# Decoder layer: the down projection's parts moved between the pairs of the next gate-up block, seven of eight pairs in seven products, some operand sums made by DMA

## The chip, the cores and the metric

The kernel runs on one core of a Trainium2 chip. A core has a matrix engine (TensorE; PE in the profile, PEld for its weight loads), VectorE (DVE), ScalarE (ACT), GpSimd (POOL) and SyncE (SP), which work side by side and wait for one another through semaphores. DMA transfers are issued from an engine's queue and carried out by 16 DMA engines. SBUF is the working memory; matmuls write into PSUM, which is used here as eight banks of 128x512 float32.

The metric is the device time of one execution in microseconds. The kernel before took 1120.58 us, the median of three runs (1119.26 to 1120.66).

## The reference

One decoder layer on x of 256 tokens by 2048 in float32: a normalised input goes through one combined projection, two groups of heads (gated linear attention and sparse attention) make the mixer's output, an output projection adds it to x, and a SwiGLU FFN of width 5632 follows. Only the last lines matter here:

```python
h = x + jnp.concatenate([gla_out, nsa_out], axis=-1) @ w_out
m = rms_norm(h, ffn_norm_g)
return h + (jax.nn.silu(m @ w_gate) * (m @ w_up)) @ w_down
```

`w_gate` and `w_up` are 2048 x 5632, `w_down` is 5632 x 2048, all float32.

## The kernel before

**Precision.** A float32 matrix is used as a high part (`hi`, a copy into the matmul type, on ACT) and a low part (`lo`, the difference, on DVE). `in_parts` (L572) makes both: ACT at L573, then DVE at L574. A product of two such matrices takes three matmuls (hi hi, hi lo, lo hi) into one bank.

**The FFN in blocks.** The FFN's width is cut into 11 blocks of 512 columns. For each block `gate_up` (L972) makes the gate and up values of both token halves, and `down` (L1065) multiplies the block's activations by 512 rows of `w_down` and adds them to the residual `h_sb`. The 16 groups of 128 rows of `w_gate` and `w_up` are taken as eight pairs (a, b).

**Eight products or seven.** A pair is a 2x2 block product: two token halves by the groups a and b by the columns gate and up. Done plainly it takes eight products of a 128x128 tile of the tokens with a 128x512 tile of weights. For the pairs named in `SEVENS` (L877) it takes seven, in the way of Strassen and Winograd: token combinations (`forms`, made once by `pair_forms` and `late_forms`) meet weight combinations made anew for each block. Of the four weight tiles ga, gb, ua, ub that `load4` (L951) fetches, three are split into parts as they are (`w`; here called A), and four sums (called B) are made first: `s1` = (gb + ub, ua + ub) in one DVE instruction at L1004, `s2` in two more (L1005, L1006), then both are split. The first three products use A, the last four B. The products go into seven banks that gather over all such pairs; an ordinary pair needs an eighth. In blocks 2 to 10 six pairs are in sevens, and pairs 6 and 7 are ordinary (`ORDERS` at L883 gives their places, fourth and last).

After the last pair in sevens (`last7`) four of the banks are read out and combined (L1029 to L1033, the evacuation); after the last pair comes the epilogue (L1042 to L1045) with silu and the product of gate and up. The activations are then turned by `turn_act` (L1051): TensorE transposes into a bank, `in_parts` into `hi` and `lo`. `down` copies the residual into four banks at a time (L1072), adds 24 matmuls for each quarter of 512 output columns and copies back (L1084).

**The order.** The main loop (L1108) emits `gate_up(f)` and then `down(f - 1)`. The generators yield after each product, and `drive` (L96) lets queued side work (`urgent`) run at a set pace in between: the turn of block f - 1 starts after `last7` of block f (L1034). The order that is emitted is a priority: when the kernel is built a planner lays down the order on each engine, and it lets a later instruction go ahead where an earlier one would not be ready by its costs. On the chip every engine then runs in that fixed order.

**Buffers.** Tiles come from slots: `fraw` (3, loaded weights), `ftwo` (4, parts), `fsum` (3, sums), `f2` (6, epilogue and forms), and `g4` (23, tokens in parts, forms, residual, activations), which has existed since the kernel's start. A slot is reused when the last reader of its tile is done. All weights are loaded from SP's queue.

## Time and profile before

| | before |
|---|---|
| median of three runs | 1120.58 us |
| the profiled execution | 1121.38 us |
| its span, first to last instruction | 1119.7 us |
| granted TensorE clock | 0.998 |
| moved by DMA | 213.47 MB, 191 GB/s |

The profile comes from one execution of its own. Busy times are shares of the span, and a busy PE counts matmuls that lie in one another's pipeline; idle time of an engine that sets nothing costs nothing. The groups of the FFN are those of L985 (gate and up), L262 (used by down, and by earlier stages), L573 and L574 (parts), L1004 to L1006 (sums). The slices show where the FFN lies: it begins at about 430 us, after 15 of 40 slices, and from there DVE is busy nearly throughout.

```profile
PE   9999999999999999999999999999999999999998
DVE  6556779876588678999998989898998999898972
ACT  6644457544476486667685867667676767667682
DMA  7665553444853354575565556566574655665562
```

The line of chain by line names the two that carry the end:

```profile
PE bank L262 50%; PE bank L985 39%; PE bank L193 2%; DMA raw<-in_w_out_dram 1%; PE bank L523 1%; PE bank L829 1%; PE bank L1058 1%; PE bank L770 1%; DMA g<-in_x_dram 1%; DVE ftwo L574 0%; DVE lo L130 0%; ACT hi L129 0%; PE bank L686 0%; PE bank L395 0%; PE bank L773 0%
```

### The profile page before, as it was taken

The page shows a single profiled execution, that of the slowest core. Times are in us where ns is not written, and L with a number is a line of the kernel's source. Part 1 is how long each engine was busy: PE and PEld are TensorE (multiplying, and loading weights), DVE is VectorE, ACT ScalarE, POOL GpSimd, SP SyncE. Part 2 cuts the span into 40 slices and gives each one's busy share as a digit, 9 for nine tenths or more (in the row PEclk, how much of TensorE's full clock was granted, in tenths as well). Part 3 has the DMA queues.
Part 4 walks back from the last instruction along what each step waited for, and adds up shares of the span by engine and source line. Part 5 has one row for each costly group of instructions (what it writes and reads, how often), then busy time and mean ns, then how long its engine had stood idle before and what let it go on. Part 6 is the DMA issues. An engine that isn't in the chain of part 4 may idle for free.

```text
span 1119.7 us, 14387 instructions
## 1 busy us (share of the span) xinstructions
PE 1110.7 (99%) x5395; PEld 918.9 (82%) x5395; DVE 935.7 (84%) x1205; ACT 719.9 (64%) x956; POOL 28.5 (3%) x67
## 2 busy tenths in 40 slices
PE   9999999999999999999999999999999999999998
PEld 8888888998778787788888888888888888888886
DVE  6556779876588678999998989898998999898972
ACT  6644457544476486667685867667676767667682
POOL 3000000101000000000000000000000000000000
PEclk9999999999999999999999999999999999999999
DMA  7665553444853354575565556566574655665562
GB/s 266 209 197 179 187 184 116 156 151 152 281 207 113 115 187 150 188 252 193 189 232 186 191 192 220 190 224 206 170 261 152 227 187 190 223 225 189 182 232 76
DMA packets 110449, 213.47 MB, mean 191 GB/s; under 512 B 5109, under 2 KB 8217, under 8 KB 110378
## 3 DMA queue, kind: packets, MB, share of 16 engines
q1 hardware_dynamic: 110378, 212.54, 56.5%
q8 instruction: 42, 0.69, 0.2%
q14 instruction: 29, 0.24, 0.1%
HBM read 210.42 MB, written 2.10 MB: 190 GB/s over the span
## 4 chain that ended last, share of the span: by engine, by line
PE 96%; DMA 2%; DVE 1%; ACT 0%; issue 0%; SPq 0%; POOL 0%; ACTq 0%; DVEq 0%
PE bank L262 50%; PE bank L985 39%; PE bank L193 2%; DMA raw<-in_w_out_dram 1%; PE bank L523 1%; PE bank L829 1%; PE bank L1058 1%; PE bank L770 1%; DMA g<-in_x_dram 1%; DVE ftwo L574 0%; DVE lo L130 0%; ACT hi L129 0%; PE bank L686 0%; PE bank L395 0%; PE bank L773 0%
## 5 line engine op out<-in xcount | busy, mean ns | idle before, releaser
L985 PE MATMUL bank<-ftwo,g 128*128 128x512 f32 x1881 | 439.4, 392 | 1.0 <-DVE ftwo L574 0.8
L985 PEld LDWEIGHTS bank<-ftwo,g 128*128 128x128 f32 x1881 | 349.3, 188 | 74.1 <-DVE ftwo L574 2.3
L262 PE MATMUL bank<-hi,g 128*128 128x512 f32 (+1 forms) x1088 | 324.6, 377 | 0.0
L574 DVE TENSOR_TENSOR ftwo<-fraw,ftwo 128x1536 fp32r<-128x1536 f32 (+1 forms) x130 | 263.1, 2036 | 12.7 <-ACT ftwo L573 12.0
L573 ACT ACTIVATE ftwo<-fraw 128x1536 fp32r<-128x1536 f32 (+1 forms) x130 | 221.0, 1713 | 63.6 <-PE bank L985 28.7
L262 PE MATMUL bank<-ftwo,g 128*128 128x512 f32 x1056 | 241.6, 389 | 0.0
L262 PEld LDWEIGHTS bank<-ftwo,g 128*128 128x128 f32 x1056 | 198.1, 188 | 41.2
L262 PEld LDWEIGHTS bank<-hi,g 128*128 128x128 f32 x1088 | 192.9, 189 | 30.8 <-issue 1.7
L130 DVE TENSOR_TENSOR lo<-raw,hi 128x1024 fp32r<-128x1024 f32 (+3 forms) x125 | 152.0, 1223 | 78.6 <-ACT hi L129 78.1
L129 ACT ACTIVATE hi<-raw 128x1024 fp32r<-128x1024 f32 (+3 forms) x125 | 131.3, 1057 | 113.1 <-PE bank L262 78.7
L262 PE MATMUL bank<-lo,g 128*128 128x512 f32 (+3 forms) x544 | 195.2, 377 | 0.6 <-DVE lo L130 0.6
L573 ACT ACTIVATE ftwo<-fsum 128x1024 fp32r<-128x1024 f32 x122 | 128.2, 1059 | 92.0 <-DVE fsum L1004 44.8
L574 DVE TENSOR_TENSOR ftwo<-fsum,ftwo 128x1024 fp32r<-128x1024 f32 x122 | 147.9, 1219 | 22.4 <-ACT ftwo L573 22.4
L262 PEld LDWEIGHTS bank<-lo,g 128*128 128x128 f32 x544 | 99.1, 189 | 16.0 <-DVE lo L130 1.2
L1004 DVE TENSOR_TENSOR fsum<-fraw 128x1024 f32<-128x1024 f32 x61 | 74.3, 1219 | 0.7 <-DMA fraw<-in_w_up_dram 0.6
L1084 ACT COPY g<-bank 128x512 f32<-128x512 f32 x80 | 45.6, 585 | 42.1 <-PE bank L262 39.8
L1072 ACT COPY bank<-g 128x512 f32<-128x512 f32 x88 | 48.3, 590 | 0.9 <-DVE g L574 0.8
L193 PE MATMUL bank<-ident,g 128*128 128x128 f32 (+2 forms) x230 | 41.0, 276 | 1.9 <-DMA g<-in_x_dram 1.1
L1005 DVE TENSOR_TENSOR fsum<-fsum,fraw 128x512 f32<-128x512 f32 x61 | 41.9, 687 | 0.8
L573 ACT ACTIVATE g<-bank 128x512 fp32r<-128x512 f32 x50 | 29.6, 599 | 19.5 <-PE bank L829 8.7
L1006 DVE TENSOR_TENSOR fsum<-fsum,fraw 128x512 f32<-128x512 f32 x61 | 41.7, 684 | 0.1
L193 PEld LDWEIGHTS bank<-ident,g 128*128 128x128 f32 (+2 forms) x230 | 30.0, 142 | 12.5 <-ACT g L910 1.9
(205 smaller groups left out, 673.2 us busy)
## 6 DMA issues: line engine op xcount, KB each, us to landing
fraw<-in_w_down_dram SPq DMA_DIRECT2D x44, 1024.0 KB, 5.1
fraw<-in_w_gate_dram SPq DMA_DIRECT2D x86, 512.0 KB, 3.8
fraw<-in_w_up_dram SPq DMA_DIRECT2D x86, 512.0 KB, 4.8
raw<-in_w_in_dram SPq DMA_DIRECT2D x36, 1024.0 KB, 5.1
raw<-in_w_out_dram SPq DMA_DIRECT2D x16, 1024.0 KB, 5.1
raw<-in_w_in_dram SPq DMA_DIRECT2D x4, 1072.0 KB
g<-in_x_dram SPq DMA_DIRECT2D x7, 512.0 KB, 8.8
raw<-in_w_in_dram SPq DMA_DIRECT2D x3, 1056.0 KB, 11.3
```

The lines of the kernel that those rows point to most:

```text
L129: act(h[:, i:i + n], r[:, k + i:k + i + n], AF.Copy)
L130: TT(o[:, i:i + n], r[:, k + i:k + i + n], f32(h[:, i:i + n]), ALU.subtract)
L193: return nc.tensor.transpose(o, i, ident[:n, :n])
L262: last["mm"] = mm(bk[t], a[:, k, t * P:(t + 1) * P], m[:, off:off + w], start=(first_ and k == 0 and i == 0), stop=(end and k == 3 and i = ...
L573: act(hi, ps, AF.Copy)
L574: TT(lo, ps, f32(hi), ALU.subtract)
L985: mm(banks[q], x, m, start=new and i == 0, stop=todo[q] == 0)
L1004: TT(s1, r[:, 1:3], r[:, 3:4].to_broadcast([P, 2, 512]), ALU.add)
L1005: TT(s2[:, 0], s1[:, 1], r[:, 1], ALU.add)
L1006: TT(s2[:, 1], s2[:, 0], r[:, 0], ALU.add)
L1072: nc.scalar.copy(banks[i][t], h_sb[2 * m + i][:, t, :])
L1084: nc.scalar.copy(h_sb[n][:, t, :], banks[i][t])
```

## The change

In blocks 2 to 10 seven pairs are in sevens instead of six; only pair 7, which comes last, stays ordinary. Pair 6 therefore gets forms (`LATE`). For pairs 0, 3 and 6 of these blocks (`ADDED`) the sum `s1` is no longer made by DVE: `added_sums` loads gb and ua into a slot from POOL's queue, and a third DMA from that queue adds ub to both. These pairs load three tiles with `load4` instead of four.

For f from 2 to 9 `down(f - 1)` is no longer emitted after `gate_up(f)` but inside it, as `down_parts`: the turn of block f - 1 lies in the second pair, its first token half in the middle and its second at the end; the third, fourth, sixth and seventh pair each hold one quarter of down, as two halves (one for each token half, 12 matmuls), again in the middle and at the end. Each half takes one bank, with a copy in and a copy out. Blocks 0, 1 and 10 keep down after `gate_up`; in block 10 the turn starts after the first pair, and what is left of the side work is emitted after each `gate_up`.

The slots: `fraw` 3 to 4, `f2` 6 to 4, `fsum` 3 to 2, two new for `fadd`; `g4` 23 to 21, with two for the gate's tiles moved to a pool that is released before the FFN.

```diff
-    g4, g2, g1, small = slot(gp, "g4", 23, LINE), slot(s2p, "g2", 13), slot(s1p, "g1", 7), slot(s1p, "sm", 12)
+    g4, g2, g1, small = slot(gp, "g4", 21, LINE), slot(s2p, "g2", 13), slot(s1p, "g1", 7), slot(s1p, "sm", 12)
+
+    g4m = slot(s2p, "g4m", 2, LINE)
     def bank():
         n_tiles[0] += 1
 ...
     def gla_gate(lr):
-        dec["f"], dec["r"] = g4([4, S]), g4([4, S])
+        dec["f"], dec["r"] = g4m([4, S]), g4m([4, S])
         nc.gpsimd.memset(dec["r"], 0.0)
         for _ in range(20):
             yield
 ...
-    SEVENS = [(0, 2, 4), (0, 2, 4, 5)] + [(0, 1, 2, 3, 4, 5) for f in range(2, NFB)]
+    SEVENS = [(0, 2, 4), (0, 2, 4, 5)] + [(0, 1, 2, 3, 4, 5, 6)] * 9
+    ADDED = [(), ()] + [(0, 3, 6)] * 9
     EARLY = (0, 2, 4, 5)
-    LATE = {0: (1, 3)}
+    LATE = {0: (1, 3, 6)}
     OLD = (1, 3)
-    ORDERS = [OLD + (0, 5, 2, 4, 6, 7), (0, 1, 2, 3, 4, 6, 5, 7)] + [(0, 1, 2, 6, 3, 4, 5, 7)] * 9
+    ORDERS = [OLD + (0, 5, 2, 4, 6, 7), (0, 1, 2, 3, 4, 6, 5, 7)] + [(0, 1, 2, 3, 4, 5, 6, 7)] * 9
     forms = {}
     turned = set()
 ...
         fr = ctx.enter_context(tc.tile_pool(name="fr", bufs=1, reuse_waits="tile"))
         fs = ctx.enter_context(tc.tile_pool(name="fs", bufs=1, reuse_waits="tile"))
         fp = ctx.enter_context(tc.tile_pool(name="fp", bufs=1, reuse_waits="tile"))
-        fw["raw"], fw["two"] = slot(fr, "fraw", 3, LINE), slot(fp, "ftwo", 4, LINE)
-        g2, small = slot(fs, "f2", 6), slot(fs, "fm", 4)
-        fw["sum"] = slot(fs, "fsum", 3, LINE)
+        fw["raw"], fw["two"] = slot(fr, "fraw", 4, LINE), slot(fp, "ftwo", 4, LINE)
+        g2, small = slot(fs, "f2", 4), slot(fs, "fm", 4)
+        fw["sum"], fw["added"] = slot(fs, "fsum", 2, LINE), slot(fs, "fadd", 2, LINE)
     def load4(parts):
         r, at = fw["raw"]([4, 512]) if fw else weight("raw", 4, 512, 3, F32), 0
         for mat, k0, nk, c0 in parts:
-            nc.sync.dma_start(r[:, at:at + nk], mat[k0 * P:(k0 + nk) * P, c0:c0 + 512].rearrange("(k p) w -> p k w", p=P))
+            nc.sync.dma_start(r[:, at:at + nk], rows_of(mat, k0, nk, c0))
             at += nk
         return r
+
+    def rows_of(mat, k0, nk, c0):
+        return mat[k0 * P:(k0 + nk) * P, c0:c0 + 512].rearrange("(k p) w -> p k w", p=P)
+
+    def added_sums(a, c0):
+
+        s = fw["added"]([2, 512])
+        gb, ua, ub = (rows_of(m[0], k, 1, c0) for m, k in ((w_gate, a + 1), (w_up, a), (w_up, a + 1)))
+        nc.gpsimd.dma_start(s[:, 0:1], gb)
+        nc.gpsimd.dma_start(s[:, 1:2], ua)
+        nc.gpsimd.dma_start(s, ub.to_broadcast([P, 2, 512]), accum_op=ALU.add)
+        return s
     def two_parts():
         w = fw["two"]([2, 4, 512], F32R)
 ...
         in_parts(hi[:, :n], lo[:, :n], src)
         return [(hi[:, k], lo[:, k]) for k in range(n)]
-    def gate_up(fb, aTs, before):
+    def gate_up(fb, aTs, before, between=None):
         banks = {}
 ...
         order, sevens = ORDERS[fb], SEVENS[fb]
         last7 = max(sevens, key=order.index)
+        free_bank = all(pair in sevens for pair in order[:order.index(last7)])
         todo = dict.fromkeys((1, 5, 6, 7), 3 * len(sevens))
         todo.update(dict.fromkeys((2, 3, 4), 3 * len(sevens) + 6 * (8 - len(sevens))))
         todo[8] = 6 * (8 - len(sevens))
 ...
             if fb == 0 and at == len(OLD):
                 ffn_pools()
             a, b = 2 * pair, 2 * pair + 1
-            r = load4([(w_gate[0], a, 2, fb * FB), (w_up[0], a, 2, fb * FB)])
             if pair in sevens:
+                added = pair in ADDED[fb]
+                if added:
+                    s1 = added_sums(a, fb * FB)
+                r = load4([(w_gate[0], a, 2, fb * FB), (w_up[0], a, 1 if added else 2, fb * FB)])
                 w = parts_of(r[:, 0:3])
-                s1, s2 = fw["sum"]([2, 512]), fw["sum"]([2, 512])
-                TT(s1, r[:, 1:3], r[:, 3:4].to_broadcast([P, 2, 512]), ALU.add)
+                if not added:
+                    s1 = fw["sum"]([2, 512])
+                    TT(s1, r[:, 1:3], r[:, 3:4].to_broadcast([P, 2, 512]), ALU.add)
+                s2 = fw["sum"]([2, 512])
                 TT(s2[:, 0], s1[:, 1], r[:, 1], ALU.add)
                 TT(s2[:, 1], s2[:, 0], r[:, 0], ALU.add)
                 f = [tuple(forms[pair][:, i, j] for i in range(2)) for j in range(4)]
 ...
                 yield 2
                 product(3, f[3], w, 2)
                 yield 2
+                if between is not None and at in TURNS:
+                    for _ in range(3):
+                        next(before)
+                elif between is not None and at in DOWNS:
+                    yield from next(between)
                 hi_, lo_ = two_parts()
                 in_parts(hi_[:, 0:2], lo_[:, 0:2], s1)
                 in_parts(hi_[:, 2:4], lo_[:, 2:4], s2)
 ...
                 for q, x, k in ((5, f[0], 0), (7, f[2], 1), (6, f[1], 2), (4, tokens(a, 1), 3)):
                     product(q, x, w, k)
                     yield 2
+                if between is not None and at in TURNS:
+                    for _ in before:
+                        pass
+                elif between is not None and at in DOWNS:
+                    yield from next(between)
             else:
-                w = parts_of(r)
+                w = parts_of(load4([(w_gate[0], a, 2, fb * FB), (w_up[0], a, 2, fb * FB)]))
                 for q, t, m in ((2, 0, 0), (3, 0, 1), (4, 1, 0), (8, 1, 1)):
                     for j in range(2):
                         product(q, tokens(a + j, t), w, 2 * m + j)
                         yield 2
+            if between is None and before is not None and (at == 0 if free_bank else pair == last7):
+                urgent.append(before)
             if pair == last7:
                 q1, q7u, q5u, q57u = (g2([512]) for _ in range(4))
                 act(q1, banks[1], AF.Copy)
 ...
                 TT(q5u, banks[5], q7u, ALU.subtract)
                 TT(q7u, banks[7], q7u, ALU.add)
                 TT(q57u, banks[5], q7u, ALU.subtract)
-                if before is not None:
-                    urgent.append(before)
         if fb == 0:
             drain(urgent)
             rms(rf, ssh)
 ...
             TT(u_, banks[uq], u_, ALU.add)
             STT(g, u_, rf[:, t:t + 1], g, ALU.mult, ALU.mult)
             gs.append(g)
-        turns[fb] = turn_act(gs, aTs)
+        turns[fb] = turn_act(gs, aTs, 1 if fb in WITHIN else 6 if fb else 0)
     turns = {}
-    def turn_act(gs, aTs):
+    WITHIN = range(1, NFB - 2)
+    TURNS, DOWNS = (1,), (2, 3, 5, 6)
+
+    def down_parts(f0, aTs):
+
+        (ah, al), = aTs
+
+        def half(n, t, ws):
+            b = bank()
+            nc.scalar.copy(b, h_sb[n][:, t, :])
+            for k in range(4):
+                for i, (x, m) in enumerate(((ah, ws[k][0]), (ah, ws[k][1]), (al, ws[k][0]))):
+                    mm(b, x[:, k, t * P:(t + 1) * P], m, start=False, stop=(k == 3 and i == 2), skip_group_check=True)
+                yield 2
+            nc.scalar.copy(h_sb[n][:, t, :], b)
+
+        for n in range(NQ):
+            ws = parts_of(load4([(w_down[0], 4 * f0, 4, n * 512)]))
+            for t in range(NT):
+                yield half(n, t, ws)
+
+    def turn_act(gs, aTs, gap):
         hi, lo = g4([4, S], F32R), g4([4, S], F32R)
         aTs.append((hi, lo))
         for t in range(NT):
 ...
                     yield
             pv = p.rearrange("p (j s) -> p j s", j=4)
             in_parts(hi[:, :, ts], lo[:, :, ts], pv)
+            for _ in range(gap if t == 0 else 0):
+                yield
     def down(f0, aTs, last):
 ...
     drive([w_out_half(1)], 6)
     acts = []
+
+    def later_parts(f):
+        yield from down_parts(f, acts[f:f + 1])
+
     for f in range(NFB):
-        drive([gate_up(f, acts, turns.get(f - 1))], 2 if f == 0 else 3)
+        inner = f - 1 in WITHIN
+        drive([gate_up(f, acts, turns.get(f - 1), later_parts(f - 1) if inner else None)], 2 if f == 0 else 3)
+        drain(urgent)
         if f == NFB - 1:
             urgent.append(turns[f])
-        if f:
+        if f and not inner:
             drive([down(f - 1, acts[f - 1:f], False)], 3)
     drive([down(NFB - 1, acts[NFB - 1:], True)], 3)
```

## The prediction

> **What bounds the kernel now.** I read the page first, for the span and the engines' shares, then the chain that ended last.
>
> ```profile
> span 1119.7 us, 14387 instructions
> PE 1110.7 (99%) x5395; PEld 918.9 (82%) x5395; DVE 935.7 (84%) x1205; ACT 719.9 (64%) x956; POOL 28.5 (3%) x67
> PE 96%; DMA 2%; DVE 1%; ACT 0%; issue 0%; SPq 0%; POOL 0%; ACTq 0%; DVEq 0%
> ```
>
> TensorE sets the end: 96% of the chain is PE. But the change touches only the FFN, so the shares must be read there. One FFN block reaches from one copy at L1029 to the next. These are two of them from the timeline, and the stretches they mark (the table of stretches: length, then busy time and count of PE, PEld, DVE, ACT, POOL, clock, DMA share, GB/s).
>
> ```profile
> 563.00 0.58 ACT L1029 ACTIVATE f<-bank 128x512 f32<-128x512 f32 x1
> 625.17 0.58 ACT L1029 ACTIVATE f<-bank 128x512 f32<-128x512 f32 x1
> 512.00:563.00 51.00, 51.00 (x226) 42.23 (x225) 50.61 (x55) 34.46 (x37) 0.00 (x0) 1.00 0.51 165
> 563.00:625.17 62.17, 62.17 (x279) 51.27 (x278) 58.83 (x55) 43.42 (x46) 0.00 (x0) 1.00 0.60 203
> 998.00:1060.70 62.70, 62.70 (x282) 51.77 (x281) 59.41 (x55) 43.79 (x47) 0.00 (x0) 1.00 0.60 201
> ```
>
> A block takes 62.17 us, PE is busy in all of it, and DVE in 58.83 (95%): 3.3 us of slack. So a product removed shortens the block only if DVE, which makes the operands, keeps up.
>
> **The gain.** The pace of PE, from the down stage of that block:
>
> ```profile
> 573.09 21.93 PE L262 MATMUL bank<-ftwo,g 128*128 128x512 f32 x96
> ```
>
> 21.93/96 = 0.228 us a matmul. Blocks 2 to 10 turn a seventh pair from eight products into seven, three matmuls each: 9 x 3 x 0.228 = **6.2 us less**, 0.68 a block. A block can at best take 61.5.
>
> **What DVE has to do.** These DVE instructions ran back to back; the distance of the starts is the true cost, since recorded times overlap by about 0.09 us.
>
> ```profile
> 553.90 1.22 DVE L1004 TENSOR_TENSOR fsum<-fraw 128x1024 f32<-128x1024 f32 x1
> 555.03 0.68 DVE L1006 TENSOR_TENSOR fsum<-fsum,fraw 128x512 f32<-128x512 f32 x1
> 555.64 1.22 DVE L574 TENSOR_TENSOR ftwo<-fsum,ftwo 128x1024 fp32r<-128x1024 f32 x1
> 556.77 1.75 DVE L574 TENSOR_TENSOR ftwo<-fraw,ftwo 128x1536 fp32r<-128x1536 f32 x1
> 558.44 1.22 DVE L574 TENSOR_TENSOR ftwo<-fsum,ftwo 128x1024 fp32r<-128x1024 f32 x1
> 559.58 0.68 DVE L1005 TENSOR_TENSOR fsum<-fsum,fraw 128x512 f32<-128x512 f32 x1
> 560.18 1.22 DVE L574 TENSOR_TENSOR ftwo<-fsum,ftwo 128x1024 fp32r<-128x1024 f32 x1
> 561.31 0.68 DVE L1006 TENSOR_TENSOR fsum<-fsum,fraw 128x512 f32<-128x512 f32 x1
> 561.92 2.28 DVE L574 TENSOR_TENSOR ftwo<-fraw,ftwo 128x2048 fp32r<-128x2048 f32 x1
> 564.12 1.22 DVE L574 TENSOR_TENSOR ftwo<-fsum,ftwo 128x1024 fp32r<-128x1024 f32 x1
> ```
>
> A pair in sevens costs 1.13 (s1) + 0.60 + 0.61 (s2) + 1.67 + 2 x 1.13 = 6.27 us of DVE beside 21 x 0.228 = 4.8 of PE; an ordinary pair or a quarter of down costs 2.20 beside 24 x 0.228 = 5.5. So sevens starve PE and down feeds it; that is why the change puts down between pairs. The sum for a block: one seven more (+6.27), one ordinary pair less (-2.20), three s1 by DMA (-3 x 1.13): **+0.68, or 59.5 us of DVE in 61.5**. Slack falls from 3.3 to 2.0 us. ACT copies the same tiles first:
>
> ```profile
> L573 ACT ACTIVATE ftwo<-fraw 128x2048 fp32r<-128x2048 f32 x69 | 131.2, 1914 | 29.6 <-DMA fraw<-in_w_down_dram 17.0 <-PE bank L985 12.2 <-DMA fraw<-in_w_up_dram 0.4
> L573 ACT ACTIVATE ftwo<-fsum 128x1024 fp32r<-128x1024 f32 x122 | 128.2, 1059 | 92.0 <-DVE fsum L1004 44.8 <-DVE fsum L1006 27.7 <-PE bank L985 13.5
> L573 ACT ACTIVATE ftwo<-fraw 128x1536 fp32r<-128x1536 f32 x61 | 90.6, 1486 | 34.0 <-DMA fraw<-in_w_up_dram 17.5 <-PE bank L985 16.5
> ```
>
> It gains 1.49 + 2 x 1.06 - 1.91 = 1.7 us, to 45 of 61.5: no bound by its sum.
>
> **How far DVE can run ahead.** Operands lie in four `ftwo` slots, before and after. At the start of block 3's pairs (PE at 594.86) DVE sat idle for want of a slot:
>
> ```profile
> 594.86 5.38 PE L985 MATMUL bank<-ftwo,g 128*128 128x512 f32 x23
> 596.63 2.36 DVE L574 TENSOR_TENSOR ftwo<-fsum,ftwo 128x1024 fp32r<-128x1024 f32 x2 [2.91 <-ACT ftwo L573]
> 626.29 1.22 DVE L574 TENSOR_TENSOR ftwo<-fsum,ftwo 128x1024 fp32r<-128x1024 f32 x1
> ```
>
> By then it had written pair 0 and the first half of pair 1. That lead is gone 32.6 us later: the last sums of the sixth seven are ready at 627.5, and PE wants them after 6 x 4.8 + 5.5 less its last six matmuls, at 627.7. Six sevens in a row just fit.
>
> **Blocks 3 to 9: one stall, taken at 0.4 us each.** With down inside, the tight place is the start of a block. There DVE owes, ahead of the first down half, the block before's epilogue and the turn as well:
>
> ```profile
> L1030 DVE TENSOR_TENSOR f<-bank,f 128x512 f32<-128x512 f32 x11 | 7.5, 684 | 0.0
> L1042 DVE TENSOR_TENSOR f<-bank,f 128x512 f32<-128x512 f32 x22 | 15.0, 681 | 0.6 <-PE bank L985 0.6
> L1044 DVE TENSOR_TENSOR f<-bank,f 128x512 f32<-128x512 f32 x22 | 15.0, 682 | 0.0
> L1045 DVE SCALAR_TENSOR_TENSOR f<-f,rf,f 128x512 f32<-128x512 f32 x22 | 16.4, 744 | 0.0
> L574 DVE TENSOR_TENSOR g<-bank,g 128x512 fp32r<-128x512 f32 x50 | 33.8, 687 | 5.6 <-ACT g L573 4.7
> L573 ACT ACTIVATE g<-bank 128x512 fp32r<-128x512 f32 x50 | 29.6, 599 | 19.5 <-PE bank L829 8.7 <-PE bank L193 7.3 <-PE bank L1058 3.2
> L1072 ACT COPY bank<-g 128x512 f32<-128x512 f32 x88 | 48.3, 590 | 0.9 <-DVE g L574 0.8
> L1084 ACT COPY g<-bank 128x512 f32<-128x512 f32 x80 | 45.6, 585 | 42.1 <-PE bank L262 39.8
> ```
>
> Less the overlap of 0.09 each: the evacuation (L1030 to L1033) costs 4 x 0.59 = 2.4, the epilogue 4 x 0.59 + 2 x 0.66 = 3.7, the turn 1.2. Count from the last down half of a block (t = 0). PE: pair 7 to 5.5, pair 0 to 10.2, pair 1 with the turn's transposes (62.17 - 270 x 0.228 = 0.6) to 15.7, first part of pair 2 to 17.8; then the first half wants its weights and a bank. DVE, in program order: from about -3.2: evacuation 2.4, B0 2.26, A1 1.67, epilogue 3.7, sums of 1 (1.2, its s1 in the idle time before), B1 2.26, A2 1.67, sums of 2 2.3, first turn 0.6, weights of down 2.2 (A the three loaded matrices, B the four sums): 20.3 us, so the weights come at 17.1, or at 18.2 where s1 of pair 1 was not done ahead. The bank is worse: seven of eight hold products, so the turn and every half share the eighth. After the turn's last transposes that bank wants ACT 0.60, DVE 0.69 and the copy in, 0.59: 1.88 and hand-overs of some 0.1 each, against the 9 x 0.228 = 2.05 of PE work in between. With nothing in the way the stall is about 0.1; with a 2.20 us DVE instruction ahead it reaches 1.8. PE runs in the order laid down at build, so all that stands behind the half waits with it. I take 0.4, nearer the low end because the order can put ready sums of pair 2 ahead of the half. Block 2 has no epilogue in front: 0. The later turn-arounds of that bank (copy out 0.59, copy in 0.59 in 2.05 or 2.7 us) cost nothing unless ACT is inside a 1.9 us instruction; that is in the upper end. Seven blocks: **+2.8, from 0.7 to 12.6**.
>
> [...]
>
> **Block 10: +3.2.** Its down comes after the pairs, so seven sevens run in a row, with an epilogue and a turn in front. DVE from t = -3.2 to pair 7's operands: 2.4 + 2.26 + 2.9 + 3.7 + 2.26 + 1.2 + (6.27 + 5.14 + 6.27 + 6.27 + 5.14) + 2.2 = 46.0, so 42.8; PE wants them at 39.6. The down stage that follows gives nothing back, since there PE is the bound. By orders, 1.5 to 4.5.
>
> **At nothing.** The sum by DMA: POOL is idle in these blocks (0.00 above), and with two slots a sum can be started over 20 us ahead of its reader (from one such pair to the next is 3 x 4.8 + 5.5). These loads land in about 5 us (first row), and the adding one waits for two of them; the other rows are waits between 563 and 1060 us:
>
> ```profile
> fraw<-in_w_up_dram SPq DMA_DIRECT2D x86, 512.0 KB, 4.8
> PEld bank L985 <- DVE ftwo L574: 0.2, 1, 0.2
> ACT ftwo L573 <- DMA fraw<-in_w_up_dram: 14.1, 8, 2.1
> ```
>
> Two landings are 10 us, twice that still fits; beyond 20 the excess would be PE's, three times a block. It can't be below nothing: PE never waited for a sum's add. Traffic rises by 3 x 768 KB a block, 203 to about 244 GB/s. The fourth `fraw` slot lets SP issue earlier, which may shorten the 1.8 us a block that ACT waits for loads; PE waited 0.2 in all of them (second row), so nothing is gained. SP's queue is otherwise as before; on POOL's, an adding DMA that waits holds only other sums. Five fewer slots elsewhere (`f2`, `fsum`) and the two `g4` moved: the evacuation waits for the turn to free `f2`, which is earlier than it was; -1 to +1 for all of it. The late forms of pair 6 add to the first down:
>
> ```profile
> 513.33 0.68 DVE L933 TENSOR_TENSOR f<-g,g 128x512 f32<-128x512 f32 x1
> 516.20 0.28 DVE L894 TENSOR_TENSOR f<-f 128x128 f32<-128x128 f32 x1
> ```
>
> That is 0.6 + 4 x 0.2 + 0.6 (the low part) = 2.0 us of DVE where it is full (50.61 of 51.00 above), less one s1, with block 2's lead as cover; 0 to +1.
>
> **Sum.** -6.2 + 2.8 + 3.2 = -0.2. The profiled execution took 1121.38 (span 1119.7), 0.8 over the median 1120.58 of the runs; so 1121.2 for such an execution and **1120.4** for the median.
>
> **Rivals.**
> 1. *PE alone.* The planner puts turn, weights and copies where they fit, stalls stay at 0.1, block 10 loses 1.5: -6.2 + 0.7 + 1.5 = -4.0, **1116.6**. For it: DVE's sum fits; before, six sevens fit with 0.2 us to spare and PE hardly waited. Against: four slots make DVE wait somewhere in a block (2.9 us above), and only 2.0 are left.
> 2. *The one bank.* The first half waits for it behind DVE in every block, others behind ACT. From 0.75 us a block on the kernel is slower (-6.2 + 3.2 + 7 x 0.75 = +2.2); at 1.2 and block 10 at 3.5 it is +5.7, **1126.3**. For it: 1.88 us of chain in 2.05, DVE 97% full. Against: DVE's order is planned, and ready sums can fill PE.
> 3. *The sums come late.* POOL's issues or the adding transfer take over 20 us; at 0.5 us for each of 27 pairs, +13.5, **1134**. Against: the landings above. [...]
>
> **Chances.** Forecast (1118.2 to 1122.8) 0.35; rival 1 0.34; rival 2 0.27; rival 3 0.04. A measurement tells some 0.2% (2.2 us) from no change, so faster 0.34, same 0.35, slower 0.31. The range 1115.5 to 1127.0 takes in rival 1 and most of rival 2; the forecast's own is 1118.2 to 1122.8.
>
> **What would show it.** 27 matmuls fewer; blocks 2 to 9 at 61.5 (rival 1), 61.9 (forecast) or above 62.6 (rival 2), with PE's gaps at L1072's copies or at the first weights of down; block 10 with PE waiting for `ftwo` by some 3 us; DVE at 96 to 97% in a block; adding DMAs landing well ahead of their sums' readers. I am wrong if block 10 runs without a gap, if PE waits at every half, or if DVE's instructions themselves get longer beside POOL.

## The result, and the profile after

The changed kernel took 1127.67 us (median of four runs, 1126.02 to 1129.83), the kernel before 1120.62 beside it: a ratio of 1.0066 (95% interval 1.0046 to 1.0087). It is slower by 7 us where no change was forecast, and just outside the range. The profiled execution is the slowest of the four, 1129.83 at a granted clock of 0.997; two others, at 1.000, took 1126.02 and 1126.74. The page's first lines and its chain:

```profile
span 1128.1 us, 14557 instructions
PE 1113.8 (99%) x5368; PEld 912.4 (81%) x5368; DVE 947.7 (84%) x1229; ACT 735.9 (65%) x975; POOL 93.4 (8%) x148
PE 91%; DMA 3%; DVE 3%; ACT 1%; issue 1%; SPq 0%; POOL 0%; ACTq 0%; DVEq 0%
```

5368 matmul records instead of 5395: the 27 are gone. Yet PE's share of the chain fell from 96% to 91%, and DMA, DVE and ACT stand in it now. To see where, I cut both spans at the copies of bank 1 out of the last seven (L1029 before, L1062 after), counted the matmuls between them, and took 0.2266 us (the common distance of two starts) off for each. What is left is the time "over", transposes included:

| stretch | before: length, matmuls, over | after: length, matmuls, over |
|---|---|---|
| FFN's start to block 0's copy | 27.76, 114, 1.93 | 30.00, 118, 3.26 |
| to block 1's copy | 49.80, 213, 1.54 | 52.74, 209, 5.38 |
| to block 2's | 61.28, 266, 1.01 | 80.78, 344, 2.83 (two downs) |
| blocks 3 to 9, each | 62.2, 270, 1.02 | 62.2 (two of 62.5), 267, 1.70 (two of 2.0) |
| to block 10's | 62.22, 270, 1.03 | 46.51, 187, 4.13 |
| from there to the end | 54.67, 232, 2.10 | 54.33, 231, 1.99 |

The balance of the two profiled executions: 27 x 0.2266 = 6.1 us gained; 5.2 lost in blocks 0 and 1 (8.64 over against 3.47), 7.2 in blocks 2 to 9, 3.1 in block 10; FFN's start 0.8 earlier and the end 0.1 shorter. Together +8.4, and the spans differ by 8.4. So the whole gain went back inside the very blocks that the change shortens, and what makes the kernel slower are the two ends: the start of the FFN and block 10.

Some of these stretches of the changed kernel (block 3, block 5, up to block 10's copy, and three pieces of the start; columns as in the prediction):

```profile
586.84:649.33 62.49, 62.47 (x277) 50.66 (x275) 58.56 (x56) 45.23 (x48) 7.13 (x9) 1.00 0.73 226
711.87:774.08 62.21, 62.21 (x277) 50.66 (x275) 59.69 (x57) 45.25 (x49) 7.11 (x9) 1.00 0.77 241
1022.91:1069.41 46.50, 44.65 (x196) 35.31 (x195) 46.03 (x48) 29.26 (x30) 3.59 (x4) 1.00 0.66 199
440.00:450.00 10.00, 10.00 (x44) 7.95 (x43) 9.14 (x9) 4.88 (x4) 2.02 (x2) 1.00 1.08 315
450.00:460.00 10.00, 7.83 (x34) 5.63 (x33) 8.03 (x9) 7.65 (x7) 0.00 (x0) 1.00 0.94 327
460.00:466.00 6.00, 4.58 (x12) 3.32 (x13) 6.00 (x5) 0.78 (x1) 0.00 (x0) 0.72 0.47 146
```

**Inside the blocks** PE seems busy throughout (62.21 of 62.21), since the records of matmuls overlap: one by itself lasts 0.39 us (L1000 at 1022.78), and the common distance of two starts is 0.2266. The table of waits between 586 and 1023 us, seven blocks, shows what the busy share hides (in total, times, longest):

```profile
POOL fadd L971 <- DMA fadd<-in_w_up_dram: 116.9, 21, 7.5
DVE fsum L1024 <- DMA fraw<-in_w_up_dram: 8.3, 7, 2.1
PEld bank L1094 <- ACT bank L1091: 7.6, 22, 0.6
DVE ftwo L576 <- ACT ftwo L575: 7.6, 15, 0.6
```

The third row is the one that counts: TensorE's weight loads for a down half waited 22 times, three a block, for ScalarE's copy of the residual into the half's bank (L1091). Before, no such row existed. DVE has 59.69 of 62.21 us of work and waits little. POOL's waits hold only other sums.

**At the start** the timeline of PE has three gaps, where the waits are for operands:

```profile
451.17 7.25 PE L1000 MATMUL bank<-ftwo,g 128*128 128x512 f32 x30 [0.71 <-DVE ftwo L576]
459.89 0.73 PE L1000 MATMUL bank<-ftwo,g 128*128 128x512 f32 x2 [1.46 <-ACT ftwo L575]
462.05 6.21 PE L1000 MATMUL bank<-ftwo,g 128*128 128x512 f32 x19 [1.43 <-DVE ftwo L576]
```

From 458.42 to 462.05 PE worked 0.73 us, and then the granted clock fell: 0.72 over 460 to 466 is one stretch of 3.41 us at half, which costs 1.7 of the 5.2 in this execution. The other 3.5 repeat: in the profiled executions of experiment 2 and of the first two kernels of experiment 6, which start the FFN in the same way, blocks 0 and 1 were 6.8 to 6.9 over without a stretch at half clock there (in that of experiment 3 even 9.0). The operands were late because their loads were. DMA issues between 433 and 466 us, after and then before (count, size, median us to landing):

```profile
fraw<-in_w_up_dram SPq DMA_DIRECT2D x8, 512.0 KB, 9.3
fraw<-in_w_gate_dram SPq DMA_DIRECT2D x7, 512.0 KB, 8.8
fadd<-in_w_up_dram POOLq DMA_DIRECT2D x2, 512.0 KB, 10.6
```

```profile
fraw<-in_w_gate_dram SPq DMA_DIRECT2D x6, 512.0 KB, 4.1
fraw<-in_w_up_dram SPq DMA_DIRECT2D x6, 512.0 KB, 4.9
```

The loads that blocks 0 and 1 need took twice as long. In the same time POOL fetched the first two sums, whose first reader, in block 2, runs at 526.67 us; and a fourth `fraw` slot lets SP issue one load more ahead. The DMA engines were full, with a share of 1.08 and 0.94 above; the same two stretches before:

```profile
440.00:450.00 10.00, 10.00 (x45) 8.01 (x44) 9.97 (x9) 5.95 (x6) 0.00 (x0) 1.00 0.65 210
450.00:460.00 10.00, 10.00 (x46) 8.12 (x45) 10.00 (x9) 5.72 (x5) 0.00 (x0) 1.00 0.71 250
```

**Block 10** has three gaps between 1059 and 1066 us, each behind ACT's copy of a late sum:

```profile
1059.25 4.66 PE L1000 MATMUL bank<-ftwo,g 128*128 128x512 f32 x19 [0.64 <-ACT ftwo L575]
1064.49 0.74 PE L1000 MATMUL bank<-ftwo,g 128*128 128x512 f32 x2 [0.57 <-ACT ftwo L575]
1065.86 6.45 PE L1000 MATMUL bank<-ftwo,g 128*128 128x512 f32 x27 [0.64 <-ACT ftwo L575]
```

There DVE is busy 46.03 of 46.50: that stretch is bound by it.

### The profile page after: what moved, and what is told of

It is laid out like the page before. It is cut to its first block, busy times and chain, and to the rows that moved or that the text cites. A ratio compares the mean times of both kernels' runs of the same rounds, so it can differ in the third digit from the quotient of the medians.

```text
span 1128.1 us, 14557 instructions
## 1 busy us (share of the span) xinstructions
PE 1113.8 (99%) x5368; PEld 912.4 (81%) x5368; DVE 947.7 (84%) x1229; ACT 735.9 (65%) x975; POOL 93.4 (8%) x148
## 4 chain that ended last, share of the span: by engine, by line
PE 91%; DMA 3%; DVE 3%; ACT 1%; issue 1%; SPq 0%; POOL 0%; ACTq 0%; DVEq 0%
PE bank L264 34%; PE bank L1000 33%; PE bank L1094 16%; PE bank L195 2%; DVE ftwo L576 2%; DMA fraw<-in_w_up_dram 2%; DMA raw<-in_w_out_dram 1%; PE bank L525 1%; PE bank L831 1%; PE bank L1110 1%; PE bank L772 1%; ACT ftwo L575 0%; DMA g<-in_x_dram 0%; DVE fsum L1024 0%; DVE lo L132 0%
## 5 line engine op out<-in xcount | busy, mean ns | idle before, releaser
L1000 PE MATMUL bank<-ftwo,g 128*128 128x512 f32 x1854 | 443.3, 393 | 6.2 <-ACT ftwo L575 4.0
L1000 PEld LDWEIGHTS bank<-ftwo,g 128*128 128x128 f32 x1854 | 346.2, 188 | 83.2 <-ACT ftwo L575 8.0
L576 DVE TENSOR_TENSOR ftwo<-fraw,ftwo 128x1536 fp32r<-128x1536 f32 (+1 forms) x130 | 259.2, 1999 | 13.1 <-ACT ftwo L575 13.0
L1094 PE MATMUL bank<-ftwo,g 128*128 128x512 f32 x768 | 188.4, 394 | 0.2 <-ACT bank L1091 0.2
L575 ACT ACTIVATE ftwo<-fsum 128x1024 fp32r<-128x1024 f32 x113 | 118.2, 1054 | 55.2 <-DVE fsum L1024 26.9
L576 DVE TENSOR_TENSOR ftwo<-fsum,ftwo 128x1024 fp32r<-128x1024 f32 x113 | 136.4, 1219 | 6.0 <-ACT ftwo L575 5.9
L1096 ACT COPY g<-bank 128x512 f32<-128x512 f32 x64 | 37.7, 588 | 64.5 <-PE bank L1094 64.5
L264 PE MATMUL bank<-ftwo,g 128*128 128x512 f32 x288 | 66.2, 390 | 0.0
L1024 DVE TENSOR_TENSOR fsum<-fraw 128x1024 f32<-128x1024 f32 x43 | 52.5, 1220 | 10.2 <-DMA fraw<-in_w_up_dram 10.1
L969 POOL DMA_DIRECT2D fadd<-in_w_gate_dram x27 | 15.8, 585 | 399.7 <-DVE ftwo L576 395.8
L1027 DVE TENSOR_TENSOR fsum<-fsum,fraw 128x512 f32<-128x512 f32 x70 | 48.1, 687 | 0.5
L971 POOL DMA_DIRECT2D fadd<-in_w_up_dram x27 | 33.2, 1231 | 142.3 <-DMA fadd<-in_w_up_dram 142.3
```

The lines of the kernel that those rows point to most:

```text
L264: last["mm"] = mm(bk[t], a[:, k, t * P:(t + 1) * P], m[:, off:off + w], start=(first_ and k == 0 and i == 0), stop=(end and k == 3 and i = ...
L575: act(hi, ps, AF.Copy)
L576: TT(lo, ps, f32(hi), ALU.subtract)
L971: nc.gpsimd.dma_start(s, ub.to_broadcast([P, 2, 512]), accum_op=ALU.add)
L1000: mm(banks[q], x, m, start=new and i == 0, stop=todo[q] == 0)
L1024: TT(s1, r[:, 1:3], r[:, 3:4].to_broadcast([P, 2, 512]), ALU.add)
```

## The experiments

The theory at this point has three parts, each with its place: sums fetched too early (start), the one bank (blocks 2 to 9), DVE (block 10). Its rivals: fewer slots or more traffic as such for the start, DVE instead of the bank inside the blocks. A time without a ratio is that of one execution, beside a kernel before of 1119.2 to 1119.4 on the same chip. In a kernel with added lines the copy into the bank (L1091) has a later number.

**1. Early sums.** Both `fadd` slots are held by dummy tiles until block 0's epilogue, so POOL's first loads can't start sooner.

```diff
+        fw["hold"] = [fw["added"]([2, 512]) for _ in range(2)]
+        for t in fw["hold"]:
+            nc.gpsimd.memset(t[:, 0, 0:1], 0.0)
 ...
+        if fb == 0:
+            for t in fw.pop("hold"):
+                nc.gpsimd.tensor_copy(t[:, 0, 0:1], gs[0][:, 0:1])
```

> Two tiles hold both fadd slots until block 0's epilogue, so the first sums by DMA start at about 470 us and not at 433. Theory 'early loads' (they crowd the first weights of the FFN, DMA share 1.08 and 0.94 between 440 and 460 us): PE's time over its matmuls in blocks 0 and 1 falls from 8.6 us to about 4 (before: 3.5) and the kernel gains 3 to 5 us, to about 1123.5. Rival 'slots' (fewer f2 and fsum slots delay blocks 0 and 1): no change, 1126 to 1129. The blocks after that stay at 62.2 us by both.

Measured: 1124.30 us, ratio 1.0045 (1.0028 to 1.0062). Over in blocks 0 and 1: 4.34 instead of 8.64, no stretch at half clock; blocks 3 to 9 are as before the hold. By the ratios the hold is worth 0.2%, some 2.4 us. Its loads and PE between 433 and 466 us:

```profile
fraw<-in_w_gate_dram SPq DMA_DIRECT2D x8, 512.0 KB, 4.2
fraw<-in_w_up_dram SPq DMA_DIRECT2D x7, 512.0 KB, 4.5
```

```profile
457.80 8.48 PE L1003 MATMUL bank<-ftwo,g 128*128 128x512 f32 x36 [1.51 <-ACT ftwo L575]
```

The landings are back at 4.2 and 4.5 us with the fourth `fraw` slot still there: it was the sums. One gap of 1.51 us for an operand remains, which the kernel before hasn't.

**2. The bank's copy in.** The half starts its bank with its first matmul instead of onto the residual, so the residual is missing from the result.

```diff
-            nc.scalar.copy(b, h_sb[n][:, t, :])
 ...
-                    mm(b, x[:, k, t * P:(t + 1) * P], m, start=False, stop=(k == 3 and i == 2), skip_group_check=True)
+                    mm(b, x[:, k, t * P:(t + 1) * P], m, start=(k == 0 and i == 0), stop=(k == 3 and i == 2), skip_group_check=True)
```

> The halves of down in blocks 2 to 9 start their bank without the residual (left out of the result), so no copy in stands between two users of the one free bank. Theory 'one bank': the gaps of 0.05 to 0.16 us at three half starts of a block, and the slower matmuls behind them, go: block period from 62.2 to about 61.7. Rival 'DVE': the halves start where DVE lets them, period stays at 62.2.

Measured: 1122.55 us. The inner blocks are 61.51 to 61.57 us long, 1.01 to 1.06 over, as before the change, and no wait of PE is left in them. So all of the 0.66 us a block hangs on that copy, and over blocks 2 to 9 it is 6.2 of the 7.2 us. DVE has the same work in a shorter block, and it suffices.

**3. DVE's work.** From block 2 on the second sums are left out, 14 DVE instructions a block (14 x 0.6 = 8.4 us).

```diff
-                s2 = fw["sum"]([2, 512])
-                TT(s2[:, 0], s1[:, 1], r[:, 1], ALU.add)
-                TT(s2[:, 1], s2[:, 0], r[:, 0], ALU.add)
+                s2 = s1
```

(blocks 0 and 1 keep theirs)

> From block 2 on the second sums are left out (the parts are made from s1 again), 1.2 us of DVE less for each pair in sevens, 8.4 us a block. Theory 'one bank': inner blocks stay near 62.2 us, as DVE was not their bound; block 10 loses its 3.1 us of extra, since there DVE was. Rival 'DVE sets the inner blocks too': their period falls to about 61.6.

Measured: 1126.66 us. The inner blocks got longer, 62.5; block 10 lost its gaps (1.25 over instead of 4.13). A stretch inside the blocks, and PE's waits there:

```profile
711.00:773.00 62.00, 61.83 (x273) 50.02 (x274) 50.57 (x42) 43.96 (x47) 7.12 (x9) 1.00 0.78 239
```

```profile
PEld bank L1096 <- ACT bank L1093: 11.3, 34, 0.6
```

DVE had 11 us to spare, and TensorE waited at the bank 34 times instead of 22. In block 5 the half at 32.3 us now has six matmuls between it and the half before, where the changed kernel has eight and no wait; why the built order came out so was not tested. DVE bounds block 10 and none of the blocks 3 to 9.

**4. Block 10 with six pairs in sevens**, in the order of before, with no sums by DMA.

```diff
-    SEVENS = [(0, 2, 4), (0, 2, 4, 5)] + [(0, 1, 2, 3, 4, 5, 6)] * 9
-    ADDED = [(), ()] + [(0, 3, 6)] * 9
+    SEVENS = [(0, 2, 4), (0, 2, 4, 5)] + [(0, 1, 2, 3, 4, 5, 6)] * 8 + [(0, 1, 2, 3, 4, 5)]
+    ADDED = [(), ()] + [(0, 3, 6)] * 8 + [()]
```

> Block 10 as in the kernel before (six pairs in sevens, its old order, no sums by DMA). Theory 'seven in a row starve PE there': block 10 loses 3.1 us of gaps and takes three matmuls more (0.7), so 2.4 us less, about 1125.2. Rival 'it is the epilogue and the turn in front of it': they stay, and the gain is under 1 us.

Measured: 1127.76 us, ratio 1.0074 (1.0059 to 1.0089): nothing gained where the theory said 2.4 us. Over up to the copy fell from 4.13 to 1.48, but the last stretch rose from 1.99 to 4.01, and there are three matmuls more. The edit gave DVE its three `s1` back, and part of the debt moved behind the mark: there PE stood 0.66 us for DVE's operand and 0.45 us for ACT's copy of the turn.

**5. The same with the sums of pairs 0, 2 and 4 by DMA**, and the hold of the first experiment.

```diff
+    ADDED = [(), ()] + [(0, 3, 6)] * 8 + [(0, 2, 4)]
```

> With the hold of the first run: block 10 with six pairs in sevens in its old order, but three of them (0, 2, 4) with sums by DMA, so that DVE has 4.1 us less to do there than with seven. Theory 'DVE is the bound of block 10': PE's time over its matmuls in the last two stretches falls from 6.2 us to about 3.5, three matmuls (0.7) more: 2 us under the hold alone. Rival 'the order at its start, whatever DVE's load': under 1 us.

Measured: 1122.69 us, 1.6 less than the hold alone: 0.30 over in block 10. But the last stretch stays at 4.10, with one gap at the first copies of the down that follows. The next kernel, which also drops the pause in that turn, has it too:

```diff
-        turns[fb] = turn_act(gs, aTs, 1 if fb in WITHIN else 6 if fb else 0)
+        turns[fb] = turn_act(gs, aTs, 1 if fb in WITHIN else 0)
```

> The hold, block 10 with six pairs in sevens and three sums by DMA, and the turn of block 9 without the pause between its token halves, so that its bank is free before down. Theory (early loads, DVE in block 10, one bank as three separate costs): the run with the first two had one gap of 1.8 us left, at down's first copy in; without it 1121.0, 0.14% over before, the rest being the one bank's 0.65 us in eight blocks. Rival: the gap moves on, 1122.7.

Measured: ratio 1.0047 (1.0031 to 1.0064), median 1124.34, where the theory said 1121.0 and the rival 1122.7; its profiled execution, at a granted clock of 1.000, took 1122.06. PE's timeline there, then ACT's:

```profile
1071.29 1.89 PE L264 MATMUL bank<-ftwo,g 128*128 128x512 f32 x7 [1.76 <-ACT bank L1132]
```

```profile
1067.74 1.92 ACT L575 ACTIVATE ftwo<-fraw 128x2048 fp32r<-128x2048 f32 x1 [2.40 <-PE bank L1003]
1069.57 0.70 ACT L1077 ACTIVATE f<-f,rf 128x512 f32<-128x512 f32 x1
1070.17 0.58 ACT L575 ACTIVATE g<-bank 128x512 fp32r<-128x512 f32 x1
1070.65 2.14 ACT L1132 COPY bank<-g 128x512 f32<-128x512 f32 x4
```

ACT, whose order is fixed, stood 2.40 us for an `ftwo` slot that PE had yet to read; the four copies (L1132) queue behind it. The turn's pause wasn't the cause. The gap stayed open to the end.

**6. The residual added elsewhere.** Three ways to be rid of the copy in while it is still added: ScalarE copies the half out, then GpSimd adds it, or an adding DMA does, or (on top of the last kernel) an adding DMA from two slots of its own, with `fraw` back at three.

```diff
-            nc.scalar.copy(b, h_sb[n][:, t, :])
 ...
-            nc.scalar.copy(h_sb[n][:, t, :], b)
+            part = g2([512])
+            nc.scalar.copy(part, b)
+            nc.gpsimd.tensor_tensor(h_sb[n][:, t, :], part, h_sb[n][:, t, :], ALU.add)
```

and in the other two, in place of the last line:

```diff
+            nc.gpsimd.dma_start(h_sb[n][:, t, :], part, accum_op=ALU.add)
```

> The halves of down start their bank without the residual, ACT copies the bank out to a spare f2 tile and GpSimd, idle otherwise, adds it to the residual. Theory 'one bank': period 61.5 us as in the run without the copy in, total 5 us less, about 1122. [...]

> The same, with the sum made by an adding DMA from the spare tile onto the residual (8 x 256 KB a block more). Theory 'one bank': period 61.5 us, about 1122. Rival 'DMA': the share of the DMA engines goes from 0.78 to about 0.9, weight loads land later than 6 us, PE waits for them: 62.5 us or more.

> As f1, with the halves of down added to the residual by DMA from two slots of their own (fraw back to 3 slots to make room). The run that borrowed f2 slots waited for them at the evacuation; theory: with slots of their own the period is 61.6 us and the time about 1116. Rival: GpSimd's queue runs in order, the adds stand behind the waits of the sums (up to 7.5 us), the halves wait for their slots: 64 us or more a block.

Measured: 1189.42, 1186.67 and 1144.29 us. With GpSimd the blocks take 67 to 73 us. Its add, and two forms of DVE, between 586 and 1015 us:

```profile
L1097 POOL TENSOR_TENSOR g<-f,g 128x512 f32<-128x512 f32 x50 | 147.3, 2949 | 113.3 <-ACT f L1096 113.3
L1027 DVE TENSOR_TENSOR fsum<-fsum,fraw 128x512 f32<-128x512 f32 x42 | 46.7, 1113 | 0.2
L576 DVE TENSOR_TENSOR ftwo<-fadd,ftwo 128x1024 fp32r<-128x1024 f32 x19 | 34.5, 1813 | 1.3 <-ACT ftwo L575 1.3
```

One add takes GpSimd 2.9 us where DVE needs 0.7, and DVE's own adds stretch from 0.69 to 1.11 and from 1.22 to 1.81 us. A third form of DVE, `ftwo<-fsum` of 128x1024, went only from 1.22 to 1.26 us; what makes the others longer was not tested. With the adding DMA the tiles were held too long. (In the first of these two kernels the granted clock was also only 0.96 between 590 and 1015 us, which costs some 17 of the 425 us.) Its waits in the two:

```profile
POOL g L1097 <- ACT f L1096: 185.0, 24, 17.9
POOL fadd L971 <- DMA fadd<-in_w_up_dram: 124.0, 19, 10.0
DVE f L1064 <- DMA g<-f: 35.6, 5, 8.2
```

```profile
POOL fadd L975 <- DMA fadd<-in_w_up_dram: 145.5, 19, 10.5
POOL g L1104 <- ACT part L1103: 130.1, 21, 11.0
```

POOL issues both in the order laid down when the kernel was built. In the first of the two it stood 185.0 us (24 times) at adds whose half was not there and 124.0 us (19 times) at sums whose loads were not: an add that waits for a half holds up the next sum, and a sum that waits for its loads holds up the add, and with it the `f2` slots that DVE wants (35.6 us in five waits). Own slots took most of that away, not all: 63.3 to 65.1 us a block.

**7. The three repairs together**, with the copy in left out.

> As f1, with the residual left out of the halves' banks in blocks 2 to 9. If the three costs add up, all that is left is the gain from the products: eight blocks x 0.68 = 5.4 us, 1121.0 - 8 x 0.65 = 1115.8, a ratio of 0.996 to 0.997 to before. Rival (a fourth cost): no faster than before.

Measured: 1118.63 us over ten runs, ratio 0.9989 (0.9978 to 1.0000), blocks of 61.5 (one of 61.75). The ratio of 0.996 to 0.997 that was expected missed, and this kernel leaves work out. Some 2 us are left in the last gap. The two profiled executions at a granted clock of 0.998, this one and that before the change, differ in span by 3.2 us (1116.4 and 1119.7), near the 3.5 us that the expectation had; why the medians differ by only 0.7 stays open beyond the lower clock that most runs of this kernel were granted.

**8. Where the halves fall.** The turn's transposes in four twos between products, on top of the hold:

```diff
+                turn_here = between is not None and at in TURNS
                 product(1, tokens(b, 0), w, 1)
                 yield 2
+                if turn_here:
+                    next(before)
                 product(2, tokens(a, 0), w, 0)
                 yield 2
+                if turn_here:
+                    next(before)
 ...
-                if between is not None and at in TURNS:
-                    for _ in range(3):
-                        next(before)
+                if turn_here:
+                    next(before)
 ...
+                    if turn_here and q in (6, 4):
+                        next(before)
                     product(q, x, w, k)
```

> With the hold: the turn's transposes in pairs between products instead of four in a row. If four in a row cost PE 0.355 us and two times two 0.27, as the starts of transposes show, a block is 0.17 us shorter in its two places: 62.03, 1.4 us in all. Rival: the later bank of the turn delays the first half of down and eats it: 62.2.

Measured: 1124.31 us, blocks of 62.2 as without. From the starts in the trace, the eight transposes took 0.55 instead of 0.71 us, but each return from transposes to products costs some 0.09 (a first matmul of 0.31 to 0.32 us), and there are four of them now, not two. One wait at a half moved from 41.3 to 30.2 us into the block, since now the half there has six matmuls in front of it and the other eight; there are still three.

Then down in pairs 3, 5, 6 and 7 of a block instead of 3, 4, 6 and 7 (on the kernel with the hold and the lighter block 10, as are the next ones):

```diff
-    TURNS, DOWNS = (1,), (2, 3, 5, 6)
+    TURNS, DOWNS = (1,), (2, 4, 5, 6)
```

> As f1, with the quarters of down in the third, fifth, sixth and seventh pair. If PE's waits are set by how close two halves follow each other, one more pair of neighbours means one more wait: 62.4 us a block; if they are set by where the planner puts ACT's copies, the period changes either way, 61.7 to 63.

> The kernel that holds the first sums and has block 10 with six pairs in sevens, with one quarter of down moved from the fourth pair to the fifth. Theory (the waits are set by where a half and ScalarE's copies fall): the inner blocks repeat the one look, 61.9 us each, and the whole is equal to the kernel before within 0.2% (ratio 0.999 to 1.002, 1119 to 1121 us). Rival (that look was one undisturbed run among disturbed ones): blocks of 62.2 again and a ratio of 1.003 to 1.006, as the kernel with the placement of the change has.

Measured: 1119.99 us in one execution; then, with an interval, 1121.26 us beside 1120.31 for the kernel before, ratio 1.0003 (0.9994 to 1.0012). Blocks of 61.9. Of the two branches of the first expectation, closeness of the halves (62.4) missed and the places of ACT's copies (61.7 to 63) held; the second expectation held. With the twos on top, and with down from the fourth pair on, `(3, 4, 5, 6)`:

> As the first of this call, with the turn's eight transposes in four twos between products instead of two fours. Theory (the gap that this gave with the other placement is at the first half, which has not moved): the transposes cost 0.16 us a block less, a gap of about that size opens at the first half, and the blocks stay at 61.9. Rival (the gap depended on the quarter that has moved): blocks of 61.7 to 61.8 and 1.2 to 1.5 us less in all than the first of this call.

> As the second, with the first quarter of down one pair later: the third, which now stands alone after the turn, and down in the fourth to seventh pairs. Theory (the first half waits for the bank that the turn has just used): with 4.8 us of products in between that gap is gone, and the blocks come to 61.6 to 61.75, the whole 1.5 to 2.5 us below the first of this call. Rival (VectorE): three pairs in sevens stand together at the start of a block without down between them, VectorE loses 1.5 us on each, and TensorE waits for ftwo there; blocks of 62.2 or more, slower than the first of this call by over 2 us.

Measured: ratios 1.0001 (0.9992 to 1.0010) and 1.0024 (1.0014 to 1.0034); blocks of 61.9 and 62.2. In the second kernel of these the length came as the theory said, but not for its reason: the twos opened no gap at the first half, their saving went into the extra returns. In the third the theory missed, and the rival had the length and only part of the reason: PE waited for `ftwo` once a block, by 0.3 us, and the bank's third wait came back. PE's waits in the inner blocks of the first and the third:

```profile
PEld bank L1100 <- ACT bank L1097: 4.2, 14, 0.3
```

```profile
PEld bank L1106 <- ACT bank L1103: 6.4, 21, 0.3
PEld bank L1003 <- ACT ftwo L575: 1.9, 7, 0.3
```

Side by side, the waits at the bank set the length of a block:

| kernel | waits at the bank in a block | block's time over |
|---|---|---|
| copy in left out (2 and 7) | 0 | 1.05 |
| down in pairs 3, 5, 6, 7 | 14 / 7 = 2 | 1.39 |
| as changed | 22 / 7 = 3.1 | 1.70 (blocks 5 to 9) |
| down in pairs 4 to 7, with the twos | 21 / 7 = 3, and one for `ftwo` | 1.71 |
| second sums left out | 34 / 7 = 4.9, and one of 0.2 for the turn | 2.02 |

That is some 0.2 us for each. In block 5 of the changed kernel one of them shows a start 0.386 us after the last, the next 0.341 after that, and then a few at 0.229 to 0.236.

The traces show two ways to such a wait. In block 5 of the changed kernel the halves that wait start at 712.00, 748.78 and 753.15 us. ACT ahead of the last two, and PE's products ahead of them:

```profile
746.27 0.59 ACT L1096 COPY g<-bank 128x512 f32<-128x512 f32 x1 [0.27 <-PE bank L1094]
746.75 1.49 ACT L575 ACTIVATE ftwo<-fraw 128x1536 fp32r<-128x1536 f32 x1
748.14 0.59 ACT L1091 COPY bank<-g 128x512 f32<-128x512 f32 x1
751.89 0.59 ACT L1096 COPY g<-bank 128x512 f32<-128x512 f32 x1 [2.18 <-PE bank L1094]
752.51 0.59 ACT L1091 COPY bank<-g 128x512 f32<-128x512 f32 x1
```

```profile
746.01 2.88 PE L1000 MATMUL bank<-ftwo,g 128*128 128x512 f32 x12
751.63 1.52 PE L1000 MATMUL bank<-ftwo,g 128*128 128x512 f32 x6
```

Before the third of these halves only six matmuls, 6 x 0.2266 = 1.36 us, lie between the two, and copy out and copy in alone take 2 x 0.59. Before the first and the second lie 14 and 12 matmuls (3.2 and 2.7 us), but there ACT copies weights between the copy out and the copy in, for 1.92 us (from 709.53 on) and for 1.49 us (second line above). With the copies back to back, eight matmuls were enough: the half at 743.29 us did not wait. Moving one quarter of down took away the place with six matmuls; two places with a weight copy in between remained, at 0.1 and 51.2 us into the block.

No kernel here that does the whole work beats the one before; the best equal it.

## Why the prediction was wrong, by its own steps

- **The gain, -6.2**: right, 6.1; 27 matmuls fewer, down's and the pairs' pace unchanged.
- **DVE, 59.5 of 61.5**: right, 59.7 of 62.2, and the second experiment shows that it fits in 61.5.
- **Block 10, +3.2**: right, 3.1, with PE behind late operands and DVE full; leaving out sums took the gaps away there. That the down stage behind it gives nothing back was right as well.
- **Blocks 3 to 9, one stall of 0.4 each, +2.8**: wrong. I looked for one stall, at the first half behind the turn, and priced DVE's instruction ahead of it; that half waited in one block of the seven, by 0.19 us. The later turn-arounds of the bank I put at nothing, on the ground that 2.05 or 2.7 us of products lie between, and left the case of ACT inside a 1.9 us instruction to the upper end of the range. The runs show three waits a block, at a cost of some 0.2 us each, all at later halves: two with that case, a weight copy of 1.92 or 1.49 us between ACT's two copies, and one where PE's order leaves only 1.36 us of products. They cost 0.66 us a block and, with block 2 (taken at 0; it went up by 1.8) and the longer blocks 3 and 4, 7.2 in all. The rival of the one bank had the right bank and half of the mechanism: others wait behind ACT, as it says, but the first half does not wait behind DVE. That its sum (1126.3) lies nearest to the result is partly luck, since it has nothing of the next point. PE waited for the bank at 22 of the 56 halves, not at each.
- **At nothing: sums by DMA and the fourth slot**: wrong, and in the profiled execution the largest single miss: 5.2 us in blocks 0 and 1, of which 1.7 is the stretch at half clock. I checked POOL's queue, the landing (an adding DMA lands in 8.7 us there, early enough) and the traffic in the middle of the FFN, where it was indeed harmless. What I didn't ask is when the two new slots are first free: at the FFN's start, where DMA was already busy at 0.65 to 0.71 and DVE was full. The rival of late sums looked at the wrong readers: not the sums came late, but the loads of others. The fourth slot was harmless: with it in place the landings came back. Holding the slots brought 4.3 of the 5.2 back in the profiled executions, 1.7 of it from the clock.
- **Fewer `f2` and `fsum` slots, late forms (-1 to +2)**: no wait for them stands out in the trace; not tested by themselves.

So the sum lacked 5.2 us at the start and 4.4 in the blocks (7.2 against 2.8). It had -0.2; with both, less 0.8 for the earlier start of the FFN, it comes to 8.6, beside the 8.4 by which the spans differ (three other terms were off by 0.1 each).

## What to carry to other kernels

Ask of every new buffer when it is first free, not only when it is first needed: here the two sums that were fetched as soon as they could be took bandwidth from the loads that were tight at that moment, which landed after 8.8 and 9.3 us instead of 4.1 and 4.9. When work is put between other work through one shared bank, count the turn-around (copy out, copy in, and whatever the copying engine does in between) against the least work that the built order leaves between two uses, not against the average, and multiply by all the uses. And a gain of 0.68 us a block can go whole into three waits of 0.2 us, which the busy share of the engine doesn't show (62.21 of 62.21 us).

## What the runs showed of the hardware that was not expected

- In the profiled execution of the changed kernel the granted clock was at half for 3.41 us from 462.33 us on, behind two gaps of 1.46 and 1.43 us with 0.73 us of TensorE's work between them. The same place came out either way in other executions: in experiment 4 (0.997 over the whole execution) a stretch of 3.41 us followed gaps of 1.50 and 0.67 us, in experiment 2 (0.998) none followed gaps of 1.46 and 1.60 us. A gap of 1.51 or 1.76 us alone (the hold; the last gap) had no such stretch in its profiled execution (1.000 in both). So the clock fell after a stretch that was not wholly idle, and it did not fall each time; what decides stays open.
- GpSimd's 128x512 add of two SBUF tiles took 2.95 us beside VectorE, and VectorE's adds of two operands, against those of the changed kernel, got up to 1.6 times longer (1113 ns against 686 at L1027; at L576 with `fsum` 1257 against 1219).
- A matmul that starts late costs more than its delay: the one behind it starts 0.337 to 0.341 us later, and several after it go at 0.229 to 0.236 instead of 0.2266 (35 such steps in block 5, 17 where the copy in was left out).
